# Hybrid latent-token backbone on one core: tile 3's first closing steps issued ahead of the odd mixer's weight splits, tile 2's transposes moved behind the third latent product

## Chip, cores, metric

One Trainium2 chip, one core. The metric is the device time of one execution in microseconds (us): the median of three timed runs. A profiled execution of the same kernel gives the trace.

## What is computed

Two layers over 256 latent tokens and 256 context tokens of width 1024. Each layer is FFN, mixer, FFN; the mixer of layer 0 ("even") is a Fourier mix beside a long convolution, that of layer 1 ("odd") is two bidirectional scans. In the last mixer and FFN only latent tokens go on. Cut to what matters here:

```
def _modulate(x, shift, scale):
    return (_ln(x) * (1.0 + scale) + shift).astype(x.dtype)

def _post_ln(x, y, g, b):
    z = ALPHA * x.astype(jnp.float32) + y.astype(jnp.float32)
    return (_ln(z) * g + b).astype(x.dtype)

def _ffn_sublayer(x, shift, scale, gate, w_in, w_out, g, b):
    a, u = jnp.split(_modulate(x, shift, scale) @ w_in, 2, axis=-1)
    y = (jax.nn.silu(a) * u) @ w_out
    return _post_ln(x, 0.5 * gate * y, g, b)
...
        x = _ffn_sublayer(x, m[:, 0], m[:, 1], m[:, 2], ...)
        h = _modulate(x, m[:, 3], m[:, 4])
        y, yc = _odd_mixer(h, hc, od_w_in[j], od_w_out[j], ...)
```

## The kernel before

The 512 tokens are four tiles of 128: tiles 0 and 1 are the latents, 2 and 3 the context. Every float32 product is made of three reduced-precision ones: each operand is split into a high part (a cast on ACT) and a low part (a subtraction on DVE), and hi·hi, hi·lo and lo·hi are accumulated in PSUM.

Weights come as units of 128x1024 through the class `Stream`: a DMA on SP's queue loads a unit into one of three `raw` buffers, the cast at L78 makes `hi` (or `whi`), the subtraction at L79 makes `lo` (or `wlo`), and only then is the raw buffer free for the next load. `split_spare(i)` does this ahead of need for units marked spare, as far as unit i.

Each engine runs its instructions in the order in which the program writes them; there is no scheduler. Between two products of a long loop `step()` takes one step of a background list `bg` of generators, `flush()` runs all that is left in it, and `due(t)` runs what was put by for tile t.

`ffn_close(l, i, ...)` ends an FFN. Tiles 0 and 1 are multiplied out first, then tiles 2 and 3, tile 3 last. `done(t, y)` is called as tile 2's and then tile 3's product is written. It splits the first weight units of the next stage, and puts a closing on the background list: `post_ln` (L331 product with the gate, L337 addition of x, L338 statistics, once per half; L342 aggregate, L233 and L234 reciprocal root on DVE and POOL, L347 and L353 or L351 gain and bias), then `norm` (statistics L304 or squares on ACT L317, aggregate L306, L233, L234, the bias `nb` at L395 or L388, and on ACT the normalised tile `xn`, L398, two halves). Then the transposes on PE (`ptr`, L411), the modulation `hm` (L428 on DVE, L430 on ACT) and the split into `hT` (L226, L227) are put by in `pend` until `due(t)`.

`ffn_close` is called three times with tiles 2 and 3, with three different stages behind it:
- (l, i) = (0, 0), then the even mixer's head (`tm_head`, products `hd`, L562), called **even head** below
- (0, 1), then the head of layer 1's first FFN (`tm_head` as well), the **FFN head**
- (1, 0), then the **odd mixer** (`odd_mixer`, L1115 on)

`tm_head` multiplies tile after tile, each with the same four weight units, 24 matmuls a tile; tile 0 takes hi·hi of all four units first. Its units 2 and 3 are split in `done(3, ...)`. Before tile 2's product it runs tile 2's transposes, before tile 3's product those of tile 3.

The odd mixer begins with four latent products for the scan's queries (`fm_lat`, `ql`, 24 matmuls of 256 columns, L1153, one weight unit each, only tiles 0 and 1 as operand), each copied out at L1160. The third and fourth unit are split in `done(3, ...)`; tile 2's transposes follow the first product (`od2`, 0), a flush the third. Two more such products follow (L1169), with tile 3's transposes between them, and then `pab` (L1183), the first product over all four tiles.

Of the kernel before, what the change touches and what calls it, by code (L numbers as in the profile page):

```python
# [102 lines left out]
def g_(n, d):  # L103
    SEEN[n] = G0.get(n, d)
    return G.get(n, G0.get(n, d))
# [23 lines left out]
def kernel(ctx: ExitStack, tc: tile.TileContext, a, out, stop=None):  # L129
# [14 lines left out]
    def S(shape, dt=F32, name="s"):  # L144
        count[0] += 1
        return sp.tile(shape, dt, tag="s", name=f"{name}{count[0]}")
# [13 lines left out]
    ws = Stream(nc, wp, "raw", 3, S, 2, 2)  # L160
# [3 lines left out]
    bg = []  # L164

    def step(n=1):
        for _ in range(n):
            while bg:
                try:
                    next(bg[0])  # L170
                    break
                except StopIteration:
                    bg.pop(0)

    def flush():
        while bg:
            step()
# [6 lines left out]
    def run_some(g, n):  # L184
        for _ in range(n):
            next(g, None)
# [15 lines left out]
    def alternate(*gens):  # L202
        gens = list(gens)
        while gens:
            g = gens.pop(0)
            try:
                next(g)
                gens.append(g)
                yield
            except StopIteration:  # L210
                pass
# [78 lines left out]
    def load_ln(ln, l, n, gate, streams=2):  # L290

        ln.append(bcast(a["ln_g"][l, n:n + 1, :], "lng"))
        yield
        ln.append(bcast(a["ln_b"][l, n:n + 1, :], "lnb"))
        ln.append([])
        for s in range(streams):
            yield
            ln[2].append(bcast(gate_d[gate, s:s + 1, :], "gate"))
        yield
# [138 lines left out]
    def close(t, y, gate, g, b, ax, eps, nxt, late=False, fine=False):  # L438


        yield from post_ln(t, y, gate, g, b, ax, eps, fine)
        if nxt is None:
            return
        xn = {}
        yield from norm(t, xn)
        if "all" not in hT:
            new_hT()
        tr = zipped(to_hT(t, 0, xn[t], *nxt), to_hT(t, 1, xn[t], *nxt))
        if late:
            pend[t] = tr  # L450
        else:
            yield from tr

    def due(t):
        if t in pend:
            run(pend.pop(t))
# [189 lines left out]
    def ffn_close(l, i, hs, nxt):  # L646


        ln = []
        loads = load_ln(ln, l, 2 * i, GATE_ROW[l, 8 if i else 2])  # L650

        def lhs(k, t):
            h = hs[t // 2][k // 2][:, k % 2]
            c = slice(P * (t % 2), P * (t % 2) + P)
            return h[:, 0, c], h[:, 1, c]

        def fill(k):
            if k % 2:
                hs[0].pop(k // 2)
                step(1)  # L660
            if k in range(10, 18, 2):
                next(loads)

        def closing(t, y, late=False):
            g, b, gates = ln
            return close(t, y, gates[t // 2], g, b, 2 * ALPHA, 4 * EPS, nxt, late, not late)

        y = tok_out(lhs, KF, (0, 1), fill)
        flush()
        hT.clear()  # L670
        k0 = key[0] = f"c{l}{i}"
        bg.append(alternate(closing(0, y[0]), closing(1, y[1])))

        def done(t, y):
            if t == 3:
                hs.clear()
            ws.split_spare(ws.pos + g_(f"{k0}a{t}", 2 * t - 3))
            if t == 3:
                flush()
            bg.append(closing(t, y, True))  # L680
            now.append(t)

        def fill(k):
            if now:
                step(g_(f"{k0}s3", 1))
            elif k >= KF - TAIL:
                step(g_(f"{k0}s2", 1))
            else:
                if k % 2:
                    hs[1].pop(k // 2)  # L690
                if k >= KF - TAIL - 3:
                    ws.split_spare(ws.pos + g_(f"{k0}b{KF - TAIL - k}", 1))
                step(g_(f"{k0}s1", 2) if k > g_(f"{k0}s0", 2) else 1)

        now = []
        tok_out(lhs, KF, (2, 3), fill, TAIL, done)


# [421 lines left out]
    def odd_mixer():  # L1120
# [5 lines left out]
        for d in range(2):  # L1126
            t = S([P, 2 * T], name="reset")
# [5 lines left out]
        def scan_view(t):  # L1133

            return t.rearrange("p (w r) -> p r w", r=4)

        def raster(t):
            return t.rearrange("p (r w) -> p r w", r=4)
# [8 lines left out]
        def fm_lat(n):  # L1147

            o = PS("ql")[:, 0:L]
            w = ws.get()  # L1150
            for m, (a_, b_) in enumerate(((0, 0), (1, 0), (0, 1))):
                for k in range(KD):
                    pe.matmul(o, lhsT=w[a_][:, P * k:P * k + P], rhs=hT[k][:, b_, 0:L], start=m + k == 0, stop=m == 2 and k == KD - 1)  # L1153
            step(n)
            return o

        qs = S([P, 4, L], name="qh")
        for i in range(4):
            o = fm_lat(g_(f"o{i}", 2))
            act.copy(scan_view(qs[:, i]), raster(o))  # L1160
            if i == g_("od2", 0):
                due(2)
            if i == g_("of", 3):
                flush()
# [243 lines left out]
        def tm_group(tiles, n):  # L1408
            y = {t: PS("tm") for t in tiles}
            for kp in range(4):  # L1410
                w = ws.get()
                for t in tiles:
                    tm_mm(y[t], w, kp, t)
                    step(n)
            return y
# [9 lines left out]
        y = tm_group(range(NT), 1)  # L1425
# [13 lines left out]
        y = tm_group(range(NT), 1)  # L1439
# [29 lines left out]
        y = tm_group(range(2), 2)  # L1469
# [426 lines left out]
    if stop == "ffn1":  # L1896
        flush()
        return dump_X()
    close_latents(*odd_mixer(), (1, 6))
    if stop == "odx":  # L1900
        flush()
# [104 lines left out]
```

## Time and profile before

| | |
|---|---|
| median of 3 runs | 1820.97 us (1820.81 to 1821.23) |
| the profiled execution's own time | 1818.72 us |
| its span, first to last instruction | 1816.9 us |
| mean granted TensorE clock | 0.983 of full |
| PE / DVE / ACT / POOL busy | 96% / 69% / 39% / 14% |

A time in the trace counts from the span's start. "Idle before" in square brackets is the time that the engine stood still ahead of an instruction, with what ended it. Between the span and the profiled execution's own time lie 1.82 us outside the trace; the median of the timed runs is 2.25 us above the profiled execution.

### The profile page before, as it was taken

To read this page: it belongs to the slowest core of one execution; us is meant where nothing else is said; L and a number is where in the kernel's file an instruction comes from. 1 tells how busy PE (TensorE), PEld (TensorE's weight loads), DVE (VectorE), ACT (ScalarE), POOL (GpSimd) and SP (SyncE) were. 2 spreads that over 40 slices of the span, in tenths; PEclk is the share of its full clock that TensorE was granted. 3 is DMA by queue.
4 is the path that set the end of the run, shared out by engine and by line. 5 is a ranking of instruction groups with operands and counts; after the bars stand their busy time and mean duration, and the time that the engine had idled before them with its cause. 6 is when DMAs were issued, how large, how long until landed. Compare 5 with 4: busy or idle time off the path is not lost. (4 is left out here: it accounts for less than half of the span.)

```text
span 1816.9 us, 21949 instructions
## 1 busy us (share of the span) xinstructions
PE 1735.9 (96%) x8212; PEld 1406.3 (77%) x8212; DVE 1253.7 (69%) x1819; ACT 716.6 (39%) x1049; POOL 254.7 (14%) x273
## 2 busy tenths in 40 slices
PE   7999999999999999999999999999998999869998
PEld 5788888877766788888887788888877778647887
DVE  6688887687688777676477677743577594656756
ACT  5532223453323442332335423333355463344443
POOL 1323311011000111111001111111011250110000
PEclk9999999999999999999999999999999999889999
DMA  9545765653124055554655455435554223535664
GB/s 330 211 180 198 254 236 213 239 177 132 71 74 158 24 201 213 188 186 173 221 187 168 165 216 201 174 102 199 197 178 145 93 82 108 162 114 208 212 211 135
DMA packets 91595, 315.10 MB, mean 173 GB/s; under 512 B 10849, under 2 KB 11585, under 8 KB 91489
## 3 DMA queue, kind: packets, MB, share of 16 engines
q1 hardware_dynamic: 86048, 297.29, 47.0%
q0 software_dynamic: 4576, 15.91, 2.7%
q8 instruction: 64, 1.05, 0.2%
q10 hardware_dynamic: 864, 0.51, 0.1%
q14 instruction: 43, 0.34, 0.1%
HBM read 308.38 MB, written 4.24 MB: 172 GB/s over the span
## 5 line engine op out<-in xcount | busy, mean ns | idle before, releaser
L79 DVE TENSOR_TENSOR wlo<-raw,whi 128x1024 fp32r<-128x1024 f32 x331 | 415.4, 1259 | 305.1 <-ACT whi L78 297.8
L78 ACT CAST whi<-raw 128x1024 fp32r<-128x1024 f32 x331 | 345.3, 1051 | 268.5 <-PE y L494 97.9
L243 DVE SCALAR_TENSOR_TENSOR mt<-mraw,cb 128x1024 bf16<-128x1024 f32 x256 | 309.6, 1249 | 3.0 <-DMA mraw<-in_mod_w_dram 3.0
L469 PE MATMUL pu<-hT,whi 128*128 128x512 f32 x1152 | 274.3, 390 | 0.0
L469 PEld LDWEIGHTS pu<-hT,whi 128*128 128x128 f32 x1152 | 215.8, 188 | 46.5 <-issue 1.0
L494 PE MATMUL y<-whi,hh 128*128 128x512 f32 x924 | 229.8, 390 | 2.9 <-ACT whi L78 2.9
L469 PE MATMUL pa<-hT,whi 128*128 128x512 f32 x960 | 228.3, 390 | 0.0
L469 PEld LDWEIGHTS pa<-hT,whi 128*128 128x128 f32 x960 | 179.6, 188 | 38.4 <-issue 0.9
L494 PEld LDWEIGHTS y<-whi,hh 128*128 128x128 f32 x924 | 172.5, 188 | 40.4 <-ACT whi L78 5.0
L226 ACT CAST hh<-sa 128x256 fp32r<-128x256 f32 x120 | 42.8, 404 | 312.1 <-DVE sa L640 312.1
L227 POOL TENSOR_TENSOR hh<-sa,hh 128x256 fp32r<-128x256 f32 x120 | 86.3, 740 | 515.9 <-ACT hh L226 484.6
L469 PE MATMUL pu<-hT,wlo 128*128 128x512 f32 x576 | 142.4, 389 | 0.4 <-DVE wlo L79 0.4
L469 PEld LDWEIGHTS pu<-hT,wlo 128*128 128x128 f32 x576 | 108.0, 188 | 23.2 <-DVE wlo L79 0.8
L494 PE MATMUL y<-wlo,hh 128*128 128x512 f32 x462 | 124.5, 391 | 0.2
L469 PE MATMUL pa<-hT,wlo 128*128 128x512 f32 x480 | 118.6, 389 | 0.0
L234 POOL TENSOR_TENSOR rstd<-rp,mhalf 128x1 f32<-128x1 f32 x42 | 36.5, 873 | 507.6 <-DVE rp L233 504.6
L79 DVE TENSOR_TENSOR lo<-raw,hi 128x1024 fp32r<-128x1024 f32 x63 | 80.4, 1290 | 38.5 <-ACT hi L78 37.9
L469 PEld LDWEIGHTS pa<-hT,wlo 128*128 128x128 f32 x480 | 90.1, 188 | 18.7
L494 PEld LDWEIGHTS y<-wlo,hh 128*128 128x128 f32 x462 | 86.6, 188 | 19.3 <-DVE wlo L79 1.5
L640 DVE TENSOR_TENSOR sa<-sa,pu 128x512 f32<-128x512 f32 x60 | 41.0, 683 | 58.0 <-PE pu L469 37.4
L78 ACT CAST hi<-raw 128x1024 fp32r<-128x1024 f32 x63 | 64.9, 1053 | 29.4 <-DMA raw<-in_ffn_out_dram 17.3
L562 PE MATMUL hd<-hi,hT 128*128 128x512 f32 x256 | 68.3, 416 | 6.5 <-ACT hT L226 3.7
(412 smaller groups left out, 2301.7 us busy)
## 6 DMA issues: line engine op xcount, KB each, us to landing
raw<-in_ffn_out_dram SPq DMA_DIRECT2D x154, 512.0 KB, 4.2
mraw<-in_mod_w_dram SPq DMA_DIRECT2D x144, 512.0 KB, 5.1
raw<-in_ffn_in_dram SPq DMA_DIRECT2D x120, 512.0 KB, 3.8
raw<-in_ffn_tm_dram SPq DMA_DIRECT2D x44, 512.0 KB, 3.3
raw<-in_od_fm_dram SPq DMA_DIRECT2D x17, 512.0 KB, 3.4
raw<-in_od_tm_dram SPq DMA_DIRECT2D x16, 512.0 KB, 3.3
raw<-in_ffn_head_dram SPq DMA_DIRECT2D x12, 512.0 KB, 4.6
raw<-in_ev_in_dram SPq DMA_DIRECT2D x12, 512.0 KB, 3.3
```

Source lines behind the costliest of these rows:

```text
L78: self.nc.scalar.copy(hi, w)
L79: self.nc.vector.tensor_tensor(lo, w, hi.bitcast(F32), op=ALU.subtract)
L226: act.copy(dst_hi, src)
L227: (lo_eng or dve).tensor_tensor(dst_lo, src, dst_hi.bitcast(F32), op=ALU.subtract)
L234: gp.tensor_tensor(dst, t, mhalf.to_broadcast([P, n]), op=ALU.pow)
L243: dve.scalar_tensor_tensor(H([P, D], BF16, "mt"), w, 1.0, cb[s], op0=ALU.mult, op1=ALU.mult, accum_out=acc[:, s, b:b + 1])
L469: pe.matmul(o, lhsT=w[a_][:, P * k:P * k + P], rhs=view(hT[k][:, b_, :]), start=n + k == 0, stop=n == 2 and k == KD - 1)
L494: pe.matmul(y[t][i], lhsT=lhs(k, t)[a_], rhs=w[b_][:, cols[t][i]], start=k + a_ + b_ == 0, stop=k == nk - 1 and b_ == 1)
L562: pe.matmul(y[u // 4], lhsT=hT[k][:, order[p_][0], P * t:P * t + P], rhs=w[u][order[p_][1]][:, 512 * kk:512 * kk + 512], start=p_ == 0 and ...
L640: dve.tensor_tensor(sa, sa, pu, op=ALU.mult)
```

## The change

In `done`, for tile 3, `flush()` now comes before `split_spare` instead of behind it, at all three places. For the odd mixer alone two steps of tile 3's closing (L331, L337, L338 of both halves) are also issued before the split. In the odd mixer tile 2's transposes are run after the third latent product (i == 2) instead of after the first.

```
         def done(t, y):
             if t == 3:
                 hs.clear()
-            ws.split_spare(ws.pos + g_(f"{k0}a{t}", 2 * t - 3))
             if t == 3:
                 flush()
-            bg.append(closing(t, y, True))
+            c = closing(t, y, True)
+            if (l, i, t) == (1, 0, 3):
+                run_some(c, 2)
+            ws.split_spare(ws.pos + g_(f"{k0}a{t}", 2 * t - 3))
+            bg.append(c)
             now.append(t)
...
             o = fm_lat(g_(f"o{i}", 2))
             act.copy(scan_view(qs[:, i]), raster(o))
-            if i == g_("od2", 0):
+            if i == 2:
                 due(2)
```

ACT at the even head, where tile 2's closing ends; `hi_3550`/`hi_3556` before and `hi_3557`/`hi_3563` now are the high parts of units 2 and 3, `xn_3541` is tile 2's normalised tile, `at_3614` the first result copied out:

```order
 L78 CAST hi_3466<-raw_3440 128x1024
 L78 CAST hi_3478<-raw_3452 128x1024
-L78 CAST hi_3550<-raw_3464 128x1024
-L78 CAST hi_3556<-raw_3476 128x1024
-L398 ACTIVATE xn_3541<-x_3526,nb_3542,rstd_3560 128x512 x2
+L398 ACTIVATE xn_3541<-x_3526,nb_3542,rstd_3548 128x512 x2
+L78 CAST hi_3557<-raw_3464 128x1024
+L78 CAST hi_3563<-raw_3476 128x1024
 L226 CAST at_3614<-hd_3575 128x512
```

The two casts stood ahead of tile 2's `xn` and now stand behind it. The FFN head has the same exchange, with the same two casts.

DVE at the same place; `z_3582` is tile 3's closing, `mv_3546` tile 2's statistics:

```order
 L306 BN_AGGR mv_3546<-st_3543 128x2
-L79 TENSOR_TENSOR lo_3551<-raw_3464,hi_3550 128x1024
-L79 TENSOR_TENSOR lo_3557<-raw_3476,hi_3556 128x1024
-L233 TENSOR_SCALAR rp_3561<-mv_3546 128x1
-L395 SCALAR_TENSOR_TENSOR nb_3542<-mv_3546,rstd_3560 128x1
+L233 TENSOR_SCALAR rp_3549<-mv_3546 128x1
+L395 SCALAR_TENSOR_TENSOR nb_3542<-mv_3546,rstd_3548 128x1
+L79 TENSOR_TENSOR lo_3558<-raw_3464,hi_3557 128x1024
+L79 TENSOR_TENSOR lo_3564<-raw_3476,hi_3563 128x1024
 L331 TENSOR_TENSOR z_3582<-y_3015,gate_2921 128x512
```

Tile 2's `rp` and `nb` come ahead of the two low parts; tile 3's closing still stands behind them here and at the FFN head.

ACT at the start of the odd mixer, before, from the second unit's cast on; `ql` are the latent products, `dev` is a pass over tile 3 that its `xn` needs:

```order
L78 CAST hi_10653<-raw_10567 128x1024
L78 CAST hi_10659<-raw_10579 128x1024
L398 ACTIVATE xn_10644<-x_10629,nb_10645,rstd_10663 128x512 x2
L1160 COPY qh_10680<-ql_10681 128x4x64
L430 ACTIVATE hm_10725<-ptr_10715,modc 128x128 x4
L430 ACTIVATE hm_10730<-ptr_10720,modc 128x128 x4
L226 CAST hT_10398<-hm_10725 128x4x128
L226 CAST hT_10398<-hm_10730 128x4x128
L1160 COPY qh_10680<-ql_10739 128x4x64
L78 CAST hi_10776<-raw_10651 128x1024
L1160 COPY qh_10680<-ql_10773 128x4x64
L317 ACTIVATE dev_10812,ss_10811<-x_10770,nm_10809 128x1024
```

And now, the same engine and place:

```order
L398 ACTIVATE xn_10644<-x_10629,nb_10645,rstd_10651 128x512 x2
L78 CAST hi_10668<-raw_10567 128x1024
L78 CAST hi_10674<-raw_10579 128x1024
L1163 COPY qh_10688<-ql_10689 128x4x64
L317 ACTIVATE dev_10755,ss_10754<-x_10720,nm_10752 128x1024
L1163 COPY qh_10688<-ql_10723 128x4x64
L78 CAST hi_10761<-raw_10666 128x1024
L1163 COPY qh_10688<-ql_10758 128x4x64
L430 ACTIVATE hm_10804<-ptr_10794,modc 128x128 x4
L430 ACTIVATE hm_10809<-ptr_10799,modc 128x128 x4
L226 CAST hT_10398<-hm_10804 128x4x128
L226 CAST hT_10398<-hm_10809 128x4x128
```

The casts of the third and fourth unit stand behind tile 2's `xn`; tile 3's `dev` stands fifth instead of twelfth, ahead of the copy of the second product, the fifth unit's cast and tile 2's modulation.

## Rows read from the trace of the kernel before

**Rows 1.** The page's busy time (share of span) and instructions of each engine.
```profile
PE 1735.9 (96%) x8212; PEld 1406.3 (77%) x8212; DVE 1253.7 (69%) x1819; ACT 716.6 (39%) x1049; POOL 254.7 (14%) x273
```

**Rows 2.** Timeline, even head, PE: start, us, instruction, count [idle before <-releaser].
```profile
417.74 3.79 PE L562 MATMUL hd<-hi,hT 128*128 128x512 f32 x16
...
423.56 0.73 PE L562 MATMUL hd<-lo,hT 128*128 128x512 f32 x2 [1.13 <-DVE lo L79]
...
429.62 1.03 PE L411 MATMUL ptr<-ident,xn 128*128 128x128 f32 x8
...
438.96 1.82 PE L411 MATMUL ptr<-ident,xn 128*128 128x128 f32 x8 [2.85 <-ACT xn L398]
```

**Rows 3.** Timeline, even head, ACT.
```profile
415.43 1.05 ACT L78 CAST hi<-raw 128x1024 fp32r<-128x1024 f32 x1 [0.75 <-DMA raw<-in_ev_tm_dram]
425.69 1.52 ACT L398 ACTIVATE xn<-x,nb,rstd 128x512 f32<-128x512 f32 x2 [9.22 <-DVE nb L395]
```

**Rows 4.** Timeline, even head, DVE.
```profile
422.33 2.31 DVE L79 TENSOR_TENSOR lo<-raw,hi 128x1024 fp32r<-128x1024 f32 x2
...
431.84 1.36 DVE L428 TENSOR_SCALAR hm<-ptr,modc 128x128 f32<-128x128 f32 x4
```

**Rows 5.** Windows: us, busy of each engine, PEclk, DMA share, GB/s.
```profile
425.70:429.10 3.40, 3.40 (x9) 2.67 (x9) 3.26 (x6) 1.98 (x3) 0.00 (x0) 0.50 0.93 324
439.40:442.80 3.40, 3.40 (x13) 2.65 (x11) 1.36 (x4) 2.19 (x7) 0.00 (x0) 0.50 0.02 5
...
1374.60:1381.40 6.80, 4.90 (x23) 4.90 (x24) 4.48 (x10) 5.71 (x13) 0.55 (x1) 0.50 0.95 323
```

**Rows 6.** Timeline, FFN head, PE.
```profile
995.72 3.79 PE L562 MATMUL hd<-hi,hT 128*128 128x512 f32 x16
```

**Rows 7.** Timeline, FFN head, ACT.
```profile
992.19 1.99 ACT L78 CAST hi<-raw 128x1024 fp32r<-128x1024 f32 x2
999.20 1.52 ACT L398 ACTIVATE xn<-x,nb,rstd 128x512 f32<-128x512 f32 x2 [5.01 <-DVE nb L395]
```

**Rows 8.** Timeline, FFN head, DVE.
```profile
995.90 2.31 DVE L79 TENSOR_TENSOR lo<-raw,hi 128x1024 fp32r<-128x1024 f32 x2
998.13 0.14 DVE L233 TENSOR_SCALAR rp<-mv 128x1 f32<-128x1 f32 x1
```

**Rows 9.** Timeline, odd mixer, PE.
```profile
1376.50 1.97 PE L411 MATMUL ptr<-ident,xn 128*128 128x128 f32 x8 [5.63 <-ACT xn L398]
...
1395.07 3.64 PE L1183 MATMUL pab<-hT,raw 128*32 128x512 f32 x32
```

**Rows 10.** Timeline, odd mixer, ACT.
```profile
1375.63 1.52 ACT L398 ACTIVATE xn<-x,nb,rstd 128x512 f32<-128x512 f32 x2 [9.49 <-DVE nb L395]
1377.06 0.60 ACT L1160 COPY qh<-ql 128x256 f32<-128x256 f32 x1
1377.71 2.90 ACT L430 ACTIVATE hm<-ptr,modc 128x128 f32<-128x128 f32 x8
1380.47 1.18 ACT L226 CAST hT<-hm 128x512 fp32r<-128x512 f32 x2
...
1386.91 1.15 ACT L317 ACTIVATE dev<-x,nm 128x1024 bf16<-128x1024 f32 x1 [0.68 <-DVE nm L315]
...
1389.20 1.53 ACT L398 ACTIVATE xn<-x,nb,rstd 128x512 f32<-128x512 f32 x2 [1.04 <-DVE nb L388]
```

**Rows 11.** Timeline, odd mixer, DVE.
```profile
1367.54 0.21 DVE L342 BATCH_NORM_AGGREGATE mv<-st 128x2 f32<-128x12 f32 x1
...
1369.57 1.28 DVE L353 SCALAR_TENSOR_TENSOR x<-z,rstd,lnb 128x1024 f32<-128x1024 f32 x1 [0.44 <-POOL rstd L234]
...
1372.34 2.31 DVE L79 TENSOR_TENSOR lo<-raw,hi 128x1024 fp32r<-128x1024 f32 x2
1374.57 0.15 DVE L233 TENSOR_SCALAR rp<-mv 128x1 f32<-128x1 f32 x1
...
1386.72 0.15 DVE L315 TENSOR_SCALAR nm<-acc 128x1 f32<-128x1 f32 x1
```

More of the change, by code (lines that the diff above doesn't have):

```diff
@@ L676, in done @@
                 hs.clear()
-            ws.split_spare(ws.pos + g_(f"{k0}a{t}", 2 * t - 3))
             if t == 3:
                 flush()
-            bg.append(closing(t, y, True))
+            c = closing(t, y, True)
+            if (l, i, t) == (1, 0, 3):
+                run_some(c, 2)
+            ws.split_spare(ws.pos + g_(f"{k0}a{t}", 2 * t - 3))
+            bg.append(c)
             now.append(t)
@@ L1160, in odd_mixer @@
             act.copy(scan_view(qs[:, i]), raster(o))
-            if i == g_("od2", 0):
+            if i == 2:
                 due(2)
```

## The prediction

> **What bounds the kernel now.** I read the page's busy shares first: PE has work in 96% of the span [rows 1], so time is won or lost where PE stands still or runs at the lower clock. Then I read, engine by engine, the timelines of the three places where the change alters the order: the even head, the FFN head and the odd mixer. At each, tile 2's `xn` on ACT ends a long stand-still of ACT, of 9.22, 5.01 and 9.49 us [rows 3, 7, 10], because it waits for a DVE chain, and the two weight casts of the units that PE needs next ran before that stand-still. They are what hides the casts today. Only in the odd mixer does PE itself wait for that `xn`, 5.63 us, and only there the clock then stands at 0.50 for 6.8 us [rows 9, 5]; that is the gap that can be won. It is followed by work without a gap up to `pab` at 1395.07 [rows 9].
>
> **Durations.** From the start of `rp` to the start of `xn` it takes 1.07 us (998.13 to 999.20 [rows 7, 8]; 1374.57 to 1375.63 gives 1.06 [rows 10, 11]), and the next instruction begins 1.43 us after `xn` (1377.06 less 1375.63 [rows 10]). A cast takes 1.05 alone and 1.0 in a row [rows 3, 7], a low part 1.15 in a row (2.31 for two [rows 4, 8, 11]). A matmul of 512 columns takes 0.227 us: 16 start within 3.63 us of a row of 3.79, whose rest is the drain of the last [rows 2]. A stretch of 3.4 us at 0.50 costs 1.7 us of PE's work.
>
> **Even head.** `rp` moves from behind the low parts to their old place, 422.4 [rows 4]. So `xn` begins at 423.5 instead of 425.69, a gain of 2.2 us for a tile whose transposes at 429.62 do not wait for it [rows 2]. The casts of units 2 and 3, the second of which ran at 415.43 [rows 3], now follow `xn`: 424.9 to 425.9 and to 426.9. PE begins tile 0 at 417.74, takes four matmuls with units 0 and 1 (0.9 us), and needs unit 2's high part at 418.65. It stands still for 7.3 us, until 425.9. Then come 20 matmuls (4.5 us), and after a gap like that the lower clock; I take one stretch of 3.4 us, 1.7 us lost. Tile 0 ends at 432.1, and twelve matmuls later (2.7 us) tile 2's transposes run at 434.8 instead of 429.62: 5.2 us late. More it is not, because the old order's own wait for a low part (1.13 us) and the slow stretch from 425.7 to 429.1 behind it fall away [rows 2, 5]. DVE's modulation of that tile began at 431.84 with DVE busy before it [rows 4]; now it follows the transposes at 435.7, 3.8 us late. All that tile 3 still needs (gain and bias, statistics, `nb`, `xn`) is queued behind it on DVE, so PE's wait for tile 3's transposes (2.85 us, then 3.4 us at the lower clock [rows 2, 5]) remains, at 442.8 instead of 438.96. **+3.8 us.**
>
> **FFN head.** The same exchange. `rp` goes to 995.9 [rows 8], `xn` to 997.0, the casts to 998.4 and 999.4; they ran from 992.19 [rows 7]. PE begins at 995.72 [rows 6], needs unit 2 at 996.6 and gets it at 999.4: 2.8 us of stand-still, about as long as the 2.85 us after which the clock was at 0.50 for 3.4 us [rows 2, 5], so 1.7 us more. That is 4.5 at most; the fourth unit costs nothing more, since its cast ends while PE is on the third. Tile 3's closing on DVE starts 2.7 us late (low parts end at 1001.7 instead of 998.2), then waits for tile 2's transposes as above and is as late as these. Little is given back, since PE meets no long wait in the old order here: I take off 0.4 for short stops ahead of those transposes and for the part of the slow stretch that falls into the stand-still. **+4.1 us.**
>
> **Odd mixer.** Removed: PE's 5.63 us, as the second product no longer stands behind tile 2's transposes. It runs from 1370.9 to 1373.7. Added: the third product needs a cast that stands behind `xn`. `rp` goes to 1372.4 [rows 11], `xn` to 1373.5, the casts to 1374.9 and 1375.9. PE waits 2.2 us, takes eight matmuls, and then needs the low part. On DVE tile 3's six closing operations come first (0.70 us each, to 1377.5), then two low parts to 1379.8: PE waits another 1.9 us. From an aggregate to the end of gain and bias it takes 3.3 us (1367.54 to 1370.85 [rows 11]), so tile 3's `nm` comes at 1383.2, 3.5 us earlier than the 1386.72 of before [rows 11]. But `dev` waits for it as the next instruction but one on ACT, which stands from 1377 to 1383.2 with the second product's copy, the fifth unit's cast, the third copy and tile 2's modulation behind it: 1.2 + 0.6 + 1.0 + 0.6 + 2.8 + 1.1 us [rows 10, 3] take it to 1390.6. DVE's `nb` stands behind the low part of tile 2's `hT`, so tile 3's `xn` begins at 1391.0 instead of 1389.20 [rows 10]. Behind it stand the sixth unit's cast and its product, which before ran under cover of the products ahead: PE waits some 2.5 us for the transposes and 0.2 for the cast and loses part of a slow stretch. `pab` begins at 1397.3: **+2.2 us**. The bounds: PE alone, with no wait and no slow stretch, would be 8.1 us earlier than before (5.63, and 2.45 as half of the 4.9 us it worked at 0.50 [rows 5]); it can't be, for tile 3's `xn` waits in the queue above. SP's loads behind the raw buffers of the third and fourth unit start about 5 us later, since their low parts end at 1378.7 and 1379.8 instead of 1373.5 and 1374.65 [rows 11]; the first is cast only at 1392.5, so this costs nothing.
>
> **A rule weighed.** Whether ACT would start a cast past a waiting `xn` decides the sum. The copy at 1377.06 [rows 10] had its product ready when PE's 5.63 us began, at 1370.87 [rows 9], and still ran behind `xn`: ACT did not pass it. [...]
>
> **The sum.** 3.8 + 4.1 + 2.2 = 10.1 us. The profiled execution would take 1818.72 + 10.1 = 1828.8; the median of the runs lies 2.25 above the profiled one, so I predict 1820.97 + 10.1, rounded to **1831.0 us**, 0.55% slower. Worked through in the same way with every slow stretch left out, in the old order and the new, the three places give 2.9, 3.1 and 2.0, in all 8.0; with one slow stretch more than I assume it is 11.8. The three stages behind are bound by PE, whose loss stays.
>
> **The rivals.**
> - The heads give back more: PE's lateness falls into its old wait for tile 3 if tile 3's chain is not itself late. In the even head 5.2 − 2.85 − 1.7 leaves 0.65; with the other two, 6.95: 1827.9. Against it: on DVE tile 3's closing stands behind the late low parts.
> - The odd mixer gains: tile 3's `nm` is 3.5 us earlier, and were `pab` to follow it the sum is 3.8 + 4.1 − 3.5 = 4.4: 1825.4. For it: 5.63 us of PE's wait do go. Against it: `dev` ahead of four pieces of ACT's work. It decides if tile 3's `xn` starts before 1387.
> - More slow stretches: after its gap of 5.63 us the odd mixer had 6.8 us at 0.50 [rows 5], not 3.4. If each of the three places gets a second stretch, 3 x 1.7 more: 1836.2.
> - Faster: ACT and DVE pass a waiting instruction. Then the heads lose nothing and gain up to the 2.2 us by which `xn` comes early, and the odd mixer wins 3.5 to 8.1: some 5.0 in all, 1816.0. It decides if a cast starts before `xn` does; the copy at 1377.06 speaks against it.
> - The change acts only in the odd mixer, and the heads stay as they are: +2.2, 1823.2. The order of both heads' ACT and DVE speaks against it.
>
> **How the numbers follow.** Forecast 0.73, heads give back more 0.09, odd mixer gains 0.06, more slow stretches 0.07, faster 0.03, odd mixer alone 0.02. The likeliest one's own range is 1828.5 to 1833.5 (8.0 and 11.8 with half a microsecond). The range for 8 in 10 reaches from the odd mixer's gain to short of the second slow stretches: 1825.4 to 1834.5. 0.2% of this kernel is 3.6 us, about what a measurement can tell from no change. Faster 0.03; within it 0.04 (odd mixer alone, and a little of the odd mixer's gain); slower 0.93.
>
> **What would show it.** After tile 0's first four matmuls PE waits 7.3 us for ACT `hi` in the even head and 2.8 us in the FFN head, each followed by granted clock 0.50. The `xn` of both comes 2.2 us earlier and the casts begin right behind it. In the odd mixer no wait of 5.6 us is left; instead PE waits about 2.2 for `hi`, 1.9 for `lo` and 2.5 for `xn`, ACT stands 6 us ahead of `dev`, and `pab` begins 2.2 us later counted from the first latent product. I am wrong if PE's wait in the even head is under 3 us, if `pab` comes earlier counted so, or if stages behind take the loss back.

## The result

The changed kernel takes **1835.26 us** (median of 4 runs, 1832.90 to 1838.66) against 1821.1 for the kernel before, timed beside it: ratio 1.0077, interval 1.0063 to 1.0091, 14.2 us slower. Run again beside other kernels it took 1838.65 (1836.88 to 1840.83, 4 runs; before 1821.07): ratio 1.0101, interval 1.0088 to 1.0115. The direction and the three places are as forecast. The size is not: 10.1 us were forecast, and 1835.26 lies 0.8 us above the upper end of the range.

### The profile page after: what moved, and what is told of

It is laid out like the page before. It is cut to its first block, busy times and chain, and to the rows that moved or that the text cites. A ratio compares the mean times of both kernels' runs of the same rounds, so it can differ in the third digit from the quotient of the medians.

```text
span 1831.1 us, 21954 instructions
## 1 busy us (share of the span) xinstructions
PE 1738.4 (95%) x8212; PEld 1408.1 (77%) x8212; DVE 1256.0 (69%) x1819; ACT 715.7 (39%) x1049; POOL 252.6 (14%) x273
## 3 DMA queue, kind: packets, MB, share of 16 engines
q8 instruction: 64, 1.05, 0.2%
## 5 line engine op out<-in xcount | busy, mean ns | idle before, releaser
L469 PEld LDWEIGHTS pu<-hT,wlo 128*128 128x128 f32 x576 | 108.1, 188 | 23.2 <-DVE wlo L79 0.8
L562 PE MATMUL hd<-hi,hT 128*128 128x512 f32 x256 | 69.8, 421 | 16.1 <-ACT hi L78 12.4
L562 PEld LDWEIGHTS hd<-hi,hT 128*128 128x128 f32 x256 | 51.0, 204 | 30.6 <-ACT hi L78 15.0
```

What stands on the lines that cost most here:

```text
L469: pe.matmul(o, lhsT=w[a_][:, P * k:P * k + P], rhs=view(hT[k][:, b_, :]), start=n + k == 0, stop=n == 2 and k == KD - 1)
L562: pe.matmul(y[u // 4], lhsT=hT[k][:, order[p_][0], P * t:P * t + P], rhs=w[u][order[p_][1]][:, 512 * kk:512 * kk + 512], start=p_ == 0 and ...
```

## The profile after

The profiled execution took 1832.90 us, its span is 1831.1, the mean granted clock 0.982. The waits of PE, the longest groups (us in total, times, longest):

```profile
PE hd L562 <- ACT hi L78: 12.4, 4, 6.9
PE y L460 <- ACT yt L226: 10.2, 1, 10.2
PE ptr L411 <- ACT xn L398: 8.2, 5, 3.2
```

The longest wait for `xn`, 5.6 us before, is down to 3.2, and a new group leads: the heads' `hi`. Of its 12.4 us, 9.5 are new (6.91 and 2.62 below); the other 2.9, in a head that the change doesn't touch (622 us in the trace of before), stood there already. Timeline of PE in the even head, after (answers to [rows 2]):

```profile
417.78 1.07 PE L562 MATMUL hd<-hi,hT 128*128 128x512 f32 x4
425.75 4.49 PE L562 MATMUL hd<-hi,hT 128*128 128x512 f32 x12 [6.91 <-ACT hi L78]
...
434.63 1.03 PE L411 MATMUL ptr<-ident,xn 128*128 128x128 f32 x8
...
444.36 1.36 PE L411 MATMUL ptr<-ident,xn 128*128 128x128 f32 x8 [3.24 <-ACT xn L398]
...
455.36 2.88 PE L469 MATMUL pu<-hT,whi 128*128 128x512 f32 x12
```

Four matmuls, then 6.91 us of stand-still. Twelve matmuls take 4.49 us, where sixteen took 3.79 [rows 2]. ACT at the same place (answers to [rows 3]):

```profile
423.25 1.52 ACT L398 ACTIVATE xn<-x,nb,rstd 128x512 f32<-128x512 f32 x2 [11.38 <-DVE nb L395]
424.67 1.98 ACT L78 CAST hi<-raw 128x1024 fp32r<-128x1024 f32 x2
```

The casts start 1.42 us behind `xn`, as forecast. DVE, and below it POOL, while tile 2 is modulated and tile 3 closed (answers to [rows 4]):

```profile
435.71 1.37 DVE L428 TENSOR_SCALAR hm<-ptr,modc 128x128 f32<-128x128 f32 x4 [1.10 <-PE ptr L411]
437.46 0.69 DVE L227 TENSOR_TENSOR hT<-hm,hT 128x512 fp32r<-128x512 f32 x1 [0.38 <-ACT hT L226]
438.07 2.33 DVE L353 SCALAR_TENSOR_TENSOR x<-z,rstd,lnb 128x1024 f32<-128x1024 f32 x1
...
438.02 1.29 POOL L227 TENSOR_TENSOR hT<-hm,hT 128x512 fp32r<-128x512 f32 x1 [4.77 <-ACT hT L226]
```

The modulation starts at 435.71, as forecast (435.7). But `x` takes 2.33 us: it starts 0.05 us after POOL's subtraction, and it is 1.05 us longer than in the kernel before. There, in the even head, `x` started first and it was POOL that took longer; in the FFN head, `x` was held in the kernel before as well, so the trace could have warned:

```profile
433.72 1.28 DVE L353 SCALAR_TENSOR_TENSOR x<-z,rstd,lnb 128x1024 f32<-128x1024 f32 x1
433.94 2.21 POOL L227 TENSOR_TENSOR hT<-hm,hT 128x512 fp32r<-128x512 f32 x1 [3.17 <-ACT hT L226]
...
1007.68 1.28 POOL L227 TENSOR_TENSOR hT<-hm,hT 128x512 fp32r<-128x512 f32 x1 [3.36 <-ACT hT L226]
1007.73 2.33 DVE L353 SCALAR_TENSOR_TENSOR x<-z,rstd,lnb 128x1024 f32<-128x1024 f32 x1
```

The FFN head and the odd mixer on PE (answers to [rows 6, 9]):

```profile
1002.39 1.07 PE L562 MATMUL hd<-hi,hT 128*128 128x512 f32 x4
1006.08 4.45 PE L562 MATMUL hd<-hi,hT 128*128 128x512 f32 x12 [2.62 <-ACT hi L78]
...
1034.76 3.79 PE L469 MATMUL pa<-hT,whi 128*128 128x512 f32 x16
...
1378.76 1.11 PE L1156 MATMUL ql<-hT,hi 128*128 128x256 f32 x8
...
1386.70 1.22 PE L1156 MATMUL ql<-hT,hi 128*128 128x256 f32 x8 [2.03 <-ACT hi L78]
1389.44 2.08 PE L1156 MATMUL ql<-hT,lo 128*128 128x256 f32 x8 [1.52 <-DVE lo L79]
...
1403.14 1.36 PE L411 MATMUL ptr<-ident,xn 128*128 128x128 f32 x8 [2.48 <-ACT xn L398]
1404.78 1.89 PE L1156 MATMUL ql<-hT,whi 128*128 128x256 f32 x8 [0.28 <-ACT whi L78]
...
1409.34 3.21 PE L1186 MATMUL pab<-hT,raw 128*32 128x512 f32 x28
```

2.62 us were forecast as 2.8; 2.03, 1.52, 2.48 and 0.28 as 2.2, 1.9, 2.5 and 0.2. ACT in the odd mixer (answers to [rows 10]):

```profile
1394.04 1.15 ACT L317 ACTIVATE dev<-x,nm 128x1024 bf16<-128x1024 f32 x1 [5.93 <-DVE nm L315]
...
1402.28 1.52 ACT L398 ACTIVATE xn<-x,nb,rstd 128x512 f32<-128x512 f32 x2 [1.39 <-DVE nb L388]
```

ACT stands 5.93 us ahead of `dev` (forecast: 6), with four pieces of other work behind it. Tile 3's `nb` on DVE stands beside another subtraction of POOL, and takes 1.23 us where it took 0.16 before:

```profile
1400.96 1.26 POOL L227 TENSOR_TENSOR hT<-hm,hT 128x512 fp32r<-128x512 f32 x1 [2.36 <-ACT hT L226]
1401.01 1.23 DVE L388 TENSOR_TENSOR nb<-nm,rstd 128x1 f32<-128x1 f32 x1
```

Windows over the matmuls that follow the stand-stills (us, busy of each engine, PEclk, DMA share, GB/s; answers to [rows 5]):

```profile
425.75:430.20 4.45, 4.45 (x13) 3.37 (x14) 4.38 (x6) 0.90 (x1) 0.00 (x0) 0.66 0.49 155
1006.08:1010.37 4.29, 4.29 (x13) 3.20 (x14) 4.22 (x5) 0.89 (x1) 0.00 (x0) 0.65 0.46 140
1389.40:1394.60 5.20, 5.16 (x25) 5.16 (x25) 4.04 (x7) 0.56 (x1) 1.52 (x1) 0.50 0.60 186
```

PEclk is the granted clock as a share of full speed: 0.66 and 0.65 in the mean of the first two stretches, with 0.50 from 425.75 to 428.00 and from 1006.08 to 1008.30 and 1.00 from 429.00 and from 1009.40 on, and 0.50 in the whole third.

**Lengths of the places.** They are read from the PE timeline between two instructions: even head from the first `hd` to the first `pu` (before 417.74 to 449.84, after 417.78 to 455.36), FFN head from the first `hd` to the first `pa`, odd start from the first `ql` to the first `pab` (1378.76 to 1409.34), between them the even mixer and the FFN behind it. The profiles of the experiments below are listed with them (us; bold: the kernel has the change at this place, unaltered):

| kernel | even head | between | FFN head | odd start |
|---|---|---|---|---|
| before | 32.10 | 545.88 | 28.18 | 27.23 |
| after | **37.58** | 547.03 | **32.37** | **30.58** |
| after, again | **38.53** | 546.24 | **34.81** | **30.21** |
| both heads alone | **38.28** | 545.07 | **36.10** | 26.86 |
| even head alone | **36.71** | 545.37 | 31.53 | 27.25 |
| FFN head alone | 29.49 | 548.87 | **32.38** | 26.85 |
| odd mixer alone | 32.12 | 542.95 | 31.56 | **29.46** |
| v1 (casts first, odd) | 32.11 | 545.82 | 28.32 | 26.27 |
| v2 (v1, steps first) | 31.69 | 546.64 | 30.07 | 30.82 |
| v3 (v1, later transposes) | 32.53 | 544.81 | 30.44 | 26.57 |
| v4 (v1, less on POOL) | 31.76 | 546.94 | 30.04 | 26.15 |

The other three kernels alter the places and are left out. One profile against one would mislead, since a place of which nothing was changed differs by up to 3.4 us. Means over the kernels with and without the change at a place: even head 37.78 (4) against 31.69 (7), **+6.1**; FFN head 33.92 (4) against 30.02 (7), **+3.9**; odd start 30.08 (3) against 27.05 (the 4 with its old order), **+3.0**; between, with and without the changed even head, 545.93 (4) against 545.99 (7), nothing. Sum 13.0.

## The experiments

In the runs that take the change apart, theory A is that the losses of the three places add up, with the sizes that the trace of the changed kernel shows; elsewhere A is what the expectation says. The rivals are named there too. Each median stands beside that of the kernel before on the same chip, which was 1820.85, 1821.01 or 1821.07.

**Both heads alone.** In `done`:
```
-            if t == 3:
+            if t == 3 and (l, i) != (1, 0):
                 flush()
             c = closing(t, y, True)
-            if (l, i, t) == (1, 0, 3):
-                run_some(c, 2)
             ws.split_spare(...)
+            if t == 3:
+                flush()
...
-            if i == 2:
+            if i == 0:
                 due(2)
```
Expected: 

> The change at the even head and the FFN head alone; the odd mixer keeps the old order. Theory A (the weight casts queued behind tile 2's xn on ACT, plus a collision of DVE's tile 3 gain-and-bias with POOL in the even head): the heads cost 5.5 and 4.2 us as in the trace of the change, with 1.2 us between the stages, some +10.9, about 1832. Rival B (the terms of the prediction are right and the rest comes from the odd mixer or from the clock): +7.9, about 1829. Rival C (the odd mixer is the loss): within 2 us of before.

Measured: 1831.70 (1830.87 to 1834.57), ratio 1.006 (1.0047 to 1.0073), +10.9 us (8.6 to 13.3); A's sum holds, and 7.9, the forecast for the two heads, lies outside. In this run's profile the two places are 6.2 and 7.9 us longer than in that of before, more than A has; 3.4 of the FFN head's come from weights that landed later, not from the change (below).

**Odd mixer alone.**
```
-            if t == 3:
+            if t == 3 and (l, i) == (1, 0):
                 flush()
...
             ws.split_spare(...)
+            if t == 3:
+                flush()
```

Expected: 

> The change at the odd mixer alone; both heads keep the old order. Theory A: pab 3.3 us later counted from the first latent product, about 1824.4; tile 3's nb takes over 1 us, beside POOL's subtraction for tile 2. Rival B: +2.2, about 1823.3. Rival D (the odd mixer gains by itself and only the heads lose): faster than before by 3 us or more.

Measured: 1823.77, ratio 1.0018 (1.0009 to 1.0027), +2.9 us; the expectation of a faster kernel falls, A and B are too close to tell apart. With the heads' 10.9 this gives 13.8, about the whole.

**Even head alone, FFN head alone.** The same with `(l, i) == (0, 0)` and `(l, i) == (0, 1)`, without `run_some`, and with the transposes at `i == 0`.

Expected of the even head: 

> The change at the even head alone; FFN head and odd mixer as before. Theory A (three losses that add up; the even head's is the one that the forecast had too small): 5.5 us slower than before, +-1 (even head +5.5 in the stage table, counted from tile 0's first matmul to pu; the DVE addition x there 2.3 us instead of 1.28), so some 1826.4. Theory B (the forecast's term was right at 3.8 and the rest of the loss comes from the run as a whole, low clock in stages that the change doesn't touch): 3.8, so 1824.7.

Measured: 1827.26 (1826.97 to 1828.04), ratio 1.0038 (1.0025 to 1.0051), +6.3 us. A holds; B's 3.8 lies below the interval (4.6 to 9.3). In its profile the even head takes 4.6 us more than in that of before, within A's 5.5 ±1, and 5.0 more than the mean of the old order; `x` takes 2.33.

Expected of the FFN head: 

> The change at the FFN head alone; even head and odd mixer as before. Theory A: 4.2 us slower than before, +-1, so some 1825.1, with PE's wait for ACT hi 2.6 us and the twelve matmuls behind it at granted clock near 0.50. Theory B (stages that are not touched lose too): 5.5 or more.

Measured: 1826.19, ratio 1.0031 (1.002 to 1.0042), +5.2 us (3.6 to 7.6). The profile is A's (place +4.20, PE's wait 2.52, the twelve matmuls 4.59 us); the time doesn't exclude B. Single places timed add up to 6.3 + 5.2 + 2.9 = 14.4.

**Casts ahead of the flush.** The whole change, but the high parts of the two units are cast before `flush()`; the low parts stay behind it.
```
             if t == 3:
+                ws.cast_spare(ws.pos + 3)
                 flush()
...
+    def cast_spare(self, i):
+        for j in range(self.n_split, i + 1):
+            if self.units[j][2]:
+                self.load_to(j)
+                self.early[j] = self.spare([P, 1024], F32R, "hi")
+                self.nc.scalar.copy(self.early[j], self.raw[j])
```
Where a cast made in this way exists, the later split uses it and makes the low part only.

Expected: 

> The whole change, but the casts of the last two weight units are issued ahead of the flush, so that on ACT they stand ahead of tile 2's xn as before the change; the low parts on DVE keep the changed order. Theory A: PE's waits for hi of 6.9 and 2.6 us in the heads go; in the even head it waits about 2 and 1 us for the low parts, the FFN head costs nothing, the odd mixer still loses 2 to 3.4 us (dev ahead of the other work on ACT): +2 to +5, 1823 to 1826. Rival E (the order of DVE, with the low parts behind nb, is the loss): still +10 or more.

Measured: 1829.37 (1826.29 to 1831.46), ratio 1.0043 (1.003 to 1.0056), +8.5 us (5.5 to 10.2): A's +2 to +5 was missed, and E's 10 or more is only at the edge. PE in this kernel, at the even head and the odd mixer:

```profile
427.00 0.73 PE L574 MATMUL hd<-lo,hT 128*128 128x512 f32 x2 [2.27 <-DVE lo L83]
428.13 0.73 PE L574 MATMUL hd<-lo,hT 128*128 128x512 f32 x2 [0.40 <-DVE lo L83]
...
1385.50 2.08 PE L1169 MATMUL ql<-hT,lo 128*128 128x256 f32 x8 [4.66 <-DVE lo L83]
```

No wait for `hi` is left at these places, so the stand-still of 6.91 was the cast behind `xn`. Next in line are the low parts on DVE: 2.67 us in the even head, 4.66 in the odd mixer, where tile 3's steps stand ahead of them. In this profile the places are 1.2, 2.2 and 3.0 us longer than in that of before; the sum, 6.4, falls short of 8.5, and the rest is not explained. The FFN head's 2.2 are again a later landing (7.96 us ahead of PE's start; v3 below, with the old order there and 7.92, takes 30.44 against 30.34 here), so at this head the casts alone were the loss, as A has it.

**Stand-still filled.** The whole change, with extra matmuls ahead of tile 0's first, whose result the first real one overwrites:
```
+                if v == 0 and t == tiles[0]:
+                    for _ in range({"c00": 26, "c01": 9}.get(k0, 0)):
+                        pe.matmul(y[0], lhsT=hT[0][:, 0, 0:P], rhs=w[0][0][:, 0:512], start=True, stop=True)
```
Expected: 

> The whole change, and in the two heads TensorE gets extra matmuls (128x512, into tile 0's own sum, which the first real one overwrites) just ahead of tile 0's first: 26 in the even head, 9 in the FFN head, some 5.9 and 2.0 us of work, less than the stand-still that they fill (6.9 and 2.6). Theory A (part of the loss is the lower clock that follows the stand-still): the twelve matmuls behind it take 2.9 instead of 4.5 us at both places, and the whole is 2 to 3.5 us faster than the changed kernel: some 1832. Theory B (the loss is the wait itself, and the clock stands low for reasons of its own): no difference from the changed kernel, or it is slower.

Measured: 1833.01 (1830.27 to 1834.17), ratio 1.0066 (1.0053 to 1.0078): 2.3 us below the first median of the changed kernel and 5.6 below the second; its interval meets that of the first and not that of the second. PE, even head and FFN head:

```profile
417.92 6.06 PE L562 MATMUL hd<-hi,hT 128*128 128x512 f32 x26
423.82 1.07 PE L565 MATMUL hd<-hi,hT 128*128 128x512 f32 x4
426.39 0.73 PE L565 MATMUL hd<-hi,hT 128*128 128x512 f32 x2 [1.50 <-ACT hi L78]
427.34 2.57 PE L565 MATMUL hd<-hi,hT 128*128 128x512 f32 x10 [0.21 <-ACT hi L78]
...
1006.72 0.80 PE L565 MATMUL hd<-hi,hT 128*128 128x512 f32 x2 [3.08 <-ACT hi L78]
1007.67 3.94 PE L565 MATMUL hd<-hi,hT 128*128 128x512 f32 x10 [0.16 <-ACT hi L78]
```

In the even head the granted clock stays at 1.00 behind the filled stand-still, and the twelve matmuls take 3.3 us in place of 4.49: there A's mechanism holds, but the place becomes only 0.7 us shorter than in the first profile of after. In the FFN head `hi` came later than the fill covered, by 3.08 us, and the low clock stayed (0.64 from 1006.70 to 1011.40). The whole lies on A's side and is not decided.

**Less on POOL (GpSimd).** The whole change; two entries of the table of engines put the low part of tile 2's second `hT` on DVE instead of POOL.
```
-G0 = {"qlh33": 1, ...
+G0 = {"c00l21": 0, "c10l21": 0, "qlh33": 1, ...
```

Expected: 

> The whole change, and the low part of tile 2's second hT (the subtraction of 128x512) at the even head and the odd mixer goes from GpSimd to VectorE. Theory A (a VectorE instruction that starts just behind a GpSimd one is held until that ends): the addition x in the even head falls from 2.33 to about 1.28 us and nb in the odd mixer from 1.23 to about 0.16, and VectorE has 0.7 us more to do ahead of each, so each chain ends some 0.4 us earlier. Theory B (they are slow for another reason, the write into SBUF or the place in the queue): both stay as long. The time of the whole can't tell 0.8 us.

DVE in this kernel, even head and odd mixer:

```profile
438.04 1.30 DVE L227 TENSOR_TENSOR hT<-hm,hT 128x512 fp32r<-128x512 f32 x2 [0.38 <-ACT hT L226]
439.25 1.28 DVE L353 SCALAR_TENSOR_TENSOR x<-z,rstd,lnb 128x1024 f32<-128x1024 f32 x1
...
1403.02 0.15 DVE L388 TENSOR_TENSOR nb<-nm,rstd 128x1 f32<-128x1 f32 x1
```

`x` takes 1.28 instead of 2.33 and `nb` 0.15 instead of 1.23, exactly A; B falls. From tile 2's transposes to those of tile 3 the even head takes 9.29 us instead of 9.73. The time, 1834.52 (2 runs), can't show so little.

**The changed kernel again.** Expected: 

> The changed kernel once more, unaltered, for a second profile. Theory A (the three losses belong to the three places and come back in each execution): even head +5 to +6, FFN head +4 to +8, odd mixer +2 to +3.5 against before's profile, 13 to 15 us slower in all, while the stages between them differ from the first profile in either direction. Theory B (the 1.15 us that the even mixer and the feed-forward behind it took longer belong to the change): again +1 there.

Measured: 1838.65, above A's range; the even head took 6.4 (also above A's), the FFN head 6.6, the odd start 3.0 us more than in the profile of before. The stages between took +0.4, not +1.2: the first profile's 1.15 doesn't come back, and B falls.

**Four versions with the heads in the old order.** In the odd mixer: both casts, flush, low parts, tile 3's steps, transposes behind the second product (v1); tile 3's steps ahead of the low parts (v2); transposes behind the third product (v3); and v1 with tile 2's second low part of `hT` on DVE in the FFN head and the odd mixer (v4). v1 against the changed kernel, with `cast_spare` as above:
```
-            if t == 3:
+            if t == 3 and (l, i) == (1, 0):
+                ws.cast_spare(ws.pos + 3)
                 flush()
             c = closing(t, y, True)
-            if (l, i, t) == (1, 0, 3):
-                run_some(c, 2)
             ws.split_spare(...)
+            if t == 3:
+                flush()
...
-            if i == 2:
+            if i == 1:
                 due(2)
```

Expected of v1: 

> Both heads in the old order. In the odd mixer the two casts first, then the flush, then the low parts, then tile 3's closing in steps as before, and tile 2's transposes behind the second product. Theory A: xn starts 2.2 us earlier at 1373.5 and PE works on the second product meanwhile, so the 5.63 us wait shrinks to under 1 us and pab comes 1 to 3 us earlier: 1818 to 1820. Rival F (tile 3's chain sets pab, and it does not start earlier): within 0.7 us of before.

Measured: 1821.31, ratio 1.0004 (0.9995 to 1.0013). PE's wait of 5.63 us fell to 0.85, as A has it, but PE now waits 1.90 for a low part and 1.18 for tile 3's `xn`. The odd start is 1 us shorter; the time shows no difference, as F has it.

Expected of v2: 

> Heads as before; odd mixer with both casts ahead of the flush and tile 2's transposes behind the second product, but tile 3's first closing steps ahead of the low parts. Against the run with the low parts ahead of these steps, which was 0.96 us shorter than before at this place: theory A (the steps on VectorE hold up the low part that TensorE waits for): TensorE waits some 4 us for lo, and the place is 2 us or more longer than there, so 1822 to 1824. Theory B (the steps cost nothing, it was the transposes behind the third product): no longer than there, 1821.

Measured: 1824.38, ratio 1.0021 (1.0011 to 1.0031), +3.3 us. A's size is right, its wait is not:

```profile
1380.96 1.22 PE L1171 MATMUL ql<-hT,lo 128*128 128x256 f32 x8 [2.06 <-DVE lo L83]
...
1392.00 2.08 PE L1171 MATMUL ql<-hT,hi 128*128 128x256 f32 x8 [5.99 <-ACT hi L82]
```

PE waits 2.06 us for `lo`, and then 5.99 for the next unit's `hi`, a cast on ACT. ACT in the same kernel:

```profile
1385.56 1.15 ACT L329 ACTIVATE dev<-x,nm 128x1024 bf16<-128x1024 f32 x1 [7.80 <-DVE nm L327]
...
1390.85 1.10 ACT L82 CAST hi<-raw 128x1024 fp32r<-128x1024 f32 x1
```

It stands 7.80 us ahead of `dev`, and that cast, with a copy and tile 2's modulation, is queued behind.

Expected of v3: 

> Heads as before; odd mixer with both casts ahead of the flush, then the low parts, then tile 3's steps; tile 2's transposes behind the third product. Theory A (only the steps ahead of the low parts cost): like the version with the transposes behind the second product, 1821 +-1, no difference from before that can be measured. Theory B (the later transposes cost): 2 us or more slower than before.

Measured: 1821.64, ratio 1.0005 (0.9996 to 1.0014). The later transposes cost nothing; A.

Expected of v4: 

> Heads in the old order; odd mixer with both casts ahead of the flush, low parts, tile 3's steps, and tile 2's transposes behind the second product; the low part of tile 2's second hT on VectorE instead of GpSimd in the FFN head and the odd mixer, so that no long VectorE instruction is held behind it. Theory A: the low part of 2.29 us and x of 2.33 us fall to 1.2 to 1.3, the odd mixer's start is 1.3 us shorter than before's, the FFN head 0.4: 1.7 us in all, 1819.3, at the edge of what can be told. Theory B: none of these chains ends last, no difference from before.

Measured: 1821.70, ratio 1.0005 (0.9994 to 1.0015). In its profile the two instructions fall as expected (1.22 and 1.28 us), the odd start is 1.1 us shorter than before's, and the time shows nothing. No version here beats the kernel before.

## Why the prediction was off in size

**Even head, 3.8 forecast: the step that failed.** Timed alone it costs 6.3 (4.6 to 9.3), by the mean lengths 6.1. Up to tile 2's transposes the forecast is close: 17.1 us from tile 0's first matmul, 16.85 in after and 17.70 in the mean of the four kernels with this order; its parts, a wait of 7.3 (6.91) and one stretch at the lower clock behind it (0.50 up to 428.00), are seen. What failed is "PE's wait for tile 3's transposes [...] remains, at 442.8 instead of 438.96": that the time from tile 2's modulation to tile 3's transposes, 7.1 us before (431.84 to 438.96 [rows 2, 4]), carries over. It became 8.65 (435.71 to 444.36). This is no accident of one execution: it is 7.12 or 7.13 in all seven profiles with the old order and 8.65 to 8.67 in all four with the new. So the 1.3 us that should have been given back there (9.34 before to 8.0) turned into a loss of 0.4 (9.73 in after). Of the 1.53 us missed, 1.05 is `x` held behind POOL, shown by the run with less on POOL; 0.38 is a wait for ACT's `hT` (437.46), absent before, when DVE started the modulation 2.2 us behind the transposes (429.62 to 431.84) and not 1.1 (434.63 to 435.71); the rest was not followed. Another 0.6 us lies in tile 2's transposes being later in the mean of four than forecast: the twelve matmuls behind PE's wait for `hi` take 5.58 us in after, again and in both heads alone, against 4.49 in after. Behind tile 3's transposes 0.5 comes back (10.3 us to the first `pu` in the mean of the four, 10.9 in before), and 0.4 of the 2.3 is before's own profile, longer than the mean of its order.

**FFN head, 4.1 forecast: right.** Wait 2.62 against 2.8, the lower clock 1.6 us (4.45 less 2.88, the twelve `pu` at 455.36) against 1.7. What I had not seen is how the head hangs on a landing. ACT's cast ahead of the chain and the casts behind it, in after:

```profile
992.32 1.04 ACT L78 CAST hi<-raw 128x1024 fp32r<-128x1024 f32 x1 [0.37 <-DMA raw<-in_ffn_head_dram]
...
1005.00 1.97 ACT L78 CAST hi<-raw 128x1024 fp32r<-128x1024 f32 x2
```

In both heads alone:

```profile
996.80 1.05 ACT L78 CAST hi<-raw 128x1024 fp32r<-128x1024 f32 x1 [1.37 <-DMA raw<-in_ffn_head_dram]
...
1009.48 1.98 ACT L78 CAST hi<-raw 128x1024 fp32r<-128x1024 f32 x2
```

From the second unit's cast, which starts as its weights land, to the casts that PE waits for it is 12.68 us in both: low part, tile 2's whole closing, `xn`. PE starts the head 10.07 us after that landing in after and 6.51 in both heads alone, and waits 2.62 and 6.18. The old order with like distances (9.93 in before, 6.57 in the odd mixer alone) takes 28.18 and 31.56 in place of 32.37 and 36.10, so the change costs 4.2 to 4.5 either way. The forecast reckoned the wait and the slow stretch, and took off only 0.4; with the late landing wait and slow stretch come to 7.9 (6.18, and twelve matmuls in 4.62), while the old order is then 3.4 longer itself, so that the term came out right owes something to the early landing in the profile it was read from. The landing explains why the profiles of this place spread; it was read from the traces and not varied by an experiment of its own.

**Odd mixer, 2.2 forecast: right within the measurement.** Timed 2.9 (1.6 to 4.9); alone its place takes 2.23 more than in the profile of before, in after 3.35. PE's 5.63 went, and the four new waits have the forecast sizes. The two mechanisms named are confirmed: in the run with the casts ahead of the flush PE waits 4.66 for a low part behind tile 3's steps, in v2 5.99 for a cast behind `dev`, and v1 and v3, with the low parts ahead of these steps, lose nothing. `nb` was held behind POOL for 1.07 us, which I had not foreseen. That the place still came out as forecast in the odd mixer alone is luck in part: there ACT's run from `dev` on starts 14.94 us behind the first latent product (forecast 15.4) and takes 6.85 us to the end of tile 2's `hT` (forecast 7.3), and these 0.9 us cancel most of the hold, so that tile 3's `xn` starts at 23.18 (forecast 23.2). In after the place is 1.1 us longer than in the odd mixer alone, and 1.0 of it is the time of the same matmuls: less PE's four waits it is 24.27 us in after, at a mean granted clock of 0.83, and less the three waits there (1.69, 1.52 and 3.00) 23.25 in the odd mixer alone. Eight matmuls of 256 columns take 1.12 us in most rows; the eight at 1406.47 take 1.91 in after, and the same eight 1.12 in the odd mixer alone.

**The rest.** By the terms: 2.3 us too little for the even head and 0.8 for the odd mixer, 0.2 too much for the FFN head, gives 13.0; timed alone, 14.4; the whole, 14.2 and 17.6. What makes the second series of the same kernel 3.4 us slower than the first stays open: before's median did not move (1821.1 and 1821.07). The granted clock of its four runs is a little lower (0.976 to 0.980 against 0.977 to 0.982), and in the second profile both heads are longer, the even head by 1.0 (its twelve matmuls take 5.58 us at a granted clock of 0.50, against 4.49 at 0.66) and the FFN head by 2.4, with its weights landing 7.84 us ahead of PE's start in place of 10.07; whether these are the cause isn't shown. Rivals: the heads did not give back more, the odd mixer did not gain, ACT and DVE passed nothing: the casts start 1.42 us behind `xn` in the even head, and in the run with the casts ahead of the flush the low parts, queued behind other work on DVE, keep PE waiting for 2.27 and 4.66 us. More stretches at the lower clock are part of what was missing, 1.0 us of the odd mixer in after, but not the 1.5 us of the even head's longer chain. The range failed because each term had bounds for the clock, and none for a chain that changes its length when it is moved.

## What to carry to other kernels

A cast or a subtraction of weights that needs nothing but a landed buffer belongs ahead of a waiting chain on its engine: in these runs neither passed one on ACT or DVE, and behind it, it inherits the rest of that chain: in the FFN head the casts came 12.7 us after the second unit's instead of 6.4 (985.79 to 992.19 in before). When a step moves in time, don't carry over the length of the chain behind it: look up what the other engines do at the new time, POOL above all. And read an unchanged place in several profiles before a difference of 3 us at a changed one is believed.

## What the runs showed of the hardware

Two DVE (VectorE) instructions, a large one and a tiny one, took longer where each started 0.05 us after a subtraction of POOL (GpSimd): `x`, of 128x1024, 2.33 in place of 1.28 us in the even head, and `nb`, of 128x1, 1.23 in place of 0.15 in the odd mixer, ending within 0.02 us of POOL's. With POOL's subtraction moved to DVE both were short again, 1.28 and 0.15. Where `x` started first, by 0.22 us, it took 1.28, and POOL's subtraction 2.21 in place of 1.29. In these pairs the one that started second took longer; what holds it was not shown. And a stand-still of PE of 2.62 us was followed by a granted clock of 0.50 as well as one of 6.91, while behind one of 1.50, after 7 us of extra and real matmuls, the clock stayed at 1.00. The length of a stand-still alone doesn't settle it: PE's wait for tile 3's `xn` in the even head was followed by 0.50 in before (2.85 us) and in after (3.24; 0.63 from 445.48 to 446.98 and 0.50 up to 449.00, where four matmuls took 1.71 us). In the FFN head alone (2.95) and in the even head alone (3.24) the same four took 1.18 and 1.17 us, as four do at a clock of 1.00 behind tile 2's transposes in after (435.42, 1.17).
